# Where the context rows of the window attention are loaded, normed and transposed

## The chip, the cores and the metric

The kernel runs on one core of a Trainium2 chip. The core has five engines with instruction queues of their own: TensorE (PE in the tables; its weight loads are shown as PEld), VectorE (DVE), ScalarE (ACT), GpSimd (POOL) and SyncE (SP, which here issues loads), and 16 DMA engines that carry them. The metric is the device time of one execution in microseconds, as the median of several runs.

## The reference

The program computes two blocks of a network, one behind the other, for 256 tokens of width 1024. The first block has two layers, each a token mixing and a mixture of 16 experts. The second begins with an attention in which the 256 tokens also attend to 256 rows of a context, `ctx`. Cut to what the change touches:

```python
def rms_norm(x, g):
    y = x * rsqrt(mean(x * x, axis=-1) + EPS)
    return y * g

def grouped_moe(h, ...):                       # first block, layers 0 and 1
    for e in range(N_EXPERTS):                 # 16 experts, two per token
        he = silu(t @ w_gate[e]) * (t @ w_up[e])
        y = y + combine[:, e:e + 1] * (he @ w_down[e])

def second_block(x, c, ctx, c_ctx, ...):       # x comes from the first block
    csh1, csc1, ... = split(silu(c_ctx) @ ada_w[0] + ada_b[0], 6)
    a_lat = rms_norm(x, norm_mix[0]) * (1 + sc1) + sh1
    a_ctx = rms_norm(ctx, norm_mix[0]) * (1 + csc1) + csh1
    qc, kc, vc = qkv_heads(a_ctx, w_qkv, ...)  # keys and values of the context rows
```

`ctx` and `c_ctx` are inputs, so `a_ctx` depends on nothing that the first block computes.

## The kernel before

Activations are held with features on partitions, as `[128, 8, 256]`: eight groups of 128 features, 256 tokens. A product in full precision is made of three: `mm3` (L539 to L541) multiplies a high and a low half of weights and activations in the combinations high-high, high-low, low-high. The halves are made by a cast on ACT (`hi`, `ch`, `hh`) and a subtraction on DVE (`lo`, `cl`, `hl`).

Weights come through a rotating ring of 1 MB slots (`wtile`, `load_w`, `load_runs`); SP issues all of these loads on one queue, each in the order in which it is written, once its slot is free and the load before it on its completion lane has landed. The ring has six slots of its own and more in the mixture of experts, where `experts.ahead` lets the loads run some two experts ahead: six loads per expert, two each of `w_gate`, `w_up` and `w_down`. A scheduler sets the order on each engine from priorities and its own estimate of when data is ready; work between two branches on an expert's count of tokens (`tc.If`, one per expert) is not moved over them, so the rows between two branches hold the end of one expert and the beginning of the next.

For each expert e the loop in `moe` issues: the loads ahead; `gate_up` (32 matmuls, L1216 and L1217) on the gathered rows `xgs[g]`, which groups of four experts share; `swiglu` (`gx`); `scatter_tab` (DVE `pw`, two transposes, `PT`); and, for the expert before, `down_mm` (L1260, L1261), `weighted` (ACT writes the high half of y, DVE the low one, L1265 and L1266) and, for the one before that, `place`, a scatter into yT (L1297). Near a group's end the rows of the next group are gathered (`features`, L1199) and evicted by ACT and DVE in turns (`gained`, L1188 and L1190) into the next `xgs` tile. These tiles have two slots (tag b8). `ps_("t")` is one PSUM bank for all the small transposes, `ps_("gu")` one for gathers and gate_up.

The context rows: at the last expert `win_loads` loads them as two loads of 128 rows, with two of weights behind (L1388 to L1392). After that expert ACT squares and sums each row (L1453), two small ACT instructions give the factor, and DVE multiplies the rows by it (L1455). In `win_attention` PE transposes them in 16 pieces into four PSUM banks (L1531), ACT and DVE apply gain and shift (`cw`, L1535 and L1537), and `split_act` makes `ch` and `cl` (L451, L452), the operands of 96 context products for keys and values. The statistics of the latent's own norm stand beside them: squares of xT, products with ones (L1560) whose issue is held until the last transpose, `cosp`, `rnorm`, then `hh` and `hl` and the keys' products of the latent.

## Time and profile before

| | |
|---|---|
| median of three runs | 1836.07 us (1834.82 to 1840.8) |
| the profiled execution's own time | 1838.44 us |
| its span, first to last instruction | 1836.6 us |
| mean granted TensorE clock | 0.978 |
| PE busy | 1722.1 us, 94% of the span |
| PE weight loads | 1308.2 us, 71% |
| DVE, ACT busy | 1017.9 us (55%), 802.4 us (44%) |
| DMA | 467.33 MB, mean 254 GB/s |

Every row below is from that one profiled execution. A row of the timeline gives start, duration, engine, line and operation, what is written from what, the count of equal instructions in a row, and in square brackets how long the engine stood idle before it and who released it. Times count from the start of the span. A granted clock of 1.00 is 2.4 GHz, 0.50 is 1.2 GHz.

### The profile page before, as it was taken

The page shows a single profiled execution, that of the slowest core. Times are in us where ns is not written, and L with a number is a line of the kernel's source. Part 1 is how long each engine was busy: PE and PEld are TensorE (multiplying, and loading weights), DVE is VectorE, ACT ScalarE, POOL GpSimd, SP SyncE. Part 2 cuts the span into 40 slices and gives each one's busy share as a digit, 9 for nine tenths or more (in the row PEclk, how much of TensorE's full clock was granted, in tenths as well). Part 3 has the DMA queues.
Part 4 walks back from the last instruction along what each step waited for, and adds up shares of the span by engine and source line. Part 5 has one row for each costly group of instructions (what it writes and reads, how often), then busy time and mean ns, then how long its engine had stood idle before and what let it go on. Part 6 is the DMA issues. An engine that isn't in the chain of part 4 may idle for free. (4 is left out here: it accounts for less than half of the span.)

```text
span 1836.6 us, 30698 instructions
## 1 busy us (share of the span) xinstructions
PE 1722.1 (94%) x12565; PEld 1308.2 (71%) x12565; DVE 1017.9 (55%) x1979; ACT 802.4 (44%) x1460; POOL 6.0 (0%) x15
## 2 busy tenths in 40 slices
PE   6999998899999999999899998889999999989998
PEld 4877798444444777789444343767898998979998
DVE  4876555222222886555322222887676667667775
ACT  4544543111112654543211112777566555456663
POOL 1000000000000000000000000000000000000000
PEclk8999999999999999999899998899999999999999
DMA  9787894797799666895699996520596727585520
GB/s 325 266 275 271 294 318 154 302 414 298 297 415 360 209 223 224 293 339 198 266 413 417 414 377 209 171 94 1 206 337 239 274 92 229 184 298 185 184 92 24
DMA packets 221185, 467.33 MB, mean 254 GB/s; under 512 B 9347, under 2 KB 138353, under 8 KB 196897
## 3 DMA queue, kind: packets, MB, share of 16 engines
q1 hardware_dynamic: 219952, 462.77, 69.3%
q8 instruction: 143, 2.34, 0.5%
q10 hardware_dynamic: 656, 1.32, 0.2%
q14 instruction: 82, 0.66, 0.1%
q0 software_dynamic: 352, 0.23, 0.1%
HBM read 463.24 MB, written 1.05 MB: 253 GB/s over the span
## 5 line engine op out<-in xcount | busy, mean ns | idle before, releaser
L539 PE MATMUL mm<-hh,hi 128*128 128x256 f32 x1568 | 452.6, 289 | 10.0 <-ACT hi L520 5.1
L541 PE MATMUL mm<-hh,lo 128*128 128x256 f32 x1568 | 447.9, 286 | 1.7 <-DVE lo L521 1.6
L540 PE MATMUL mm<-hl,hi 128*128 128x256 f32 x1568 | 447.4, 285 | 1.5 <-DVE hl L463 0.7
L521 DVE TENSOR_TENSOR lo<-w,hi 128x1024 fp32r<-128x1024 f32 (+4 forms) x330 | 366.0, 1127 | 97.6 <-ACT hi L520 96.7
L520 ACT CAST hi<-w 128x1024 fp32r<-128x1024 f32 (+4 forms) x330 | 310.1, 970 | 246.9 <-PE mm L540 193.2
L539 PEld LDWEIGHTS mm<-hh,hi 128*128 128x128 f32 x1568 | 301.9, 193 | 21.9 <-ACT hi L520 7.9
L541 PEld LDWEIGHTS mm<-hh,lo 128*128 128x128 f32 x1568 | 301.7, 192 | 4.3 <-DVE lo L521 2.3
L540 PEld LDWEIGHTS mm<-hl,hi 128*128 128x128 f32 x1568 | 301.7, 192 | 4.2 <-DVE hl L463 1.6
L1216 PE MATMUL ps<-w,xg 128*64 128x512 f32 x512 | 230.8, 605 | 9.2 <-ACT xg L1188 6.9
L1217 PE MATMUL ps<-w,xg 128*64 128x512 f32 x512 | 230.9, 605 | 0.0
L1216 PEld LDWEIGHTS ps<-w,xg 128*64 128x64 f32 x512 | 69.8, 139 | 151.3 <-issue 138.7
L1234 DVE TENSOR_TENSOR gx<-gx,ps 64x512 f32<-64x512 f32 (+1 forms) x35 | 23.4, 668 | 223.6 <-ACT gx L1233 185.0
L1233 ACT ACTIVATE gx<-ps 64x512 f32<-64x512 f32 (+1 forms) x35 | 20.0, 572 | 216.0 <-PE ps L1217 213.1
L1261 PE MATMUL ps<-w,he 128*64 128x512 f32 x240 | 112.8, 610 | 0.0
L1260 PE MATMUL ps<-w,he 128*64 128x512 f32 x240 | 112.1, 609 | 0.0
L378 PE MATMUL ps<-w,crep 128*32 128x512 f32 x768 | 105.3, 604 | 2.2 <-DMA w<-in_ada_w_dram 1.4
L540 PE MATMUL yT<-zl,hi 128*128 128x256 f32 x352 | 99.3, 282 | 0.0
L541 PE MATMUL yT<-zh,lo 128*128 128x256 f32 x352 | 99.2, 282 | 0.0
L539 PE MATMUL yT<-zh,hi 128*128 128x256 f32 x352 | 99.2, 282 | 0.0
L539 PE MATMUL mm<-half,hi 128*128 128x256 f32 x320 | 93.4, 292 | 0.0
L540 PE MATMUL mm<-half,hi 128*128 128x256 f32 x320 | 91.3, 285 | 0.0
L541 PE MATMUL mm<-half,lo 128*128 128x256 f32 x320 | 90.7, 283 | 0.0
(477 smaller groups left out, 2823.6 us busy)
## 6 DMA issues: line engine op xcount, KB each, us to landing
w<-in_ada_w_dram SPq DMA_DIRECT2D x96, 1024.0 KB, 7.0
w<-in_w_gate_dram SPq DMA_DIRECT2D x64, 1024.0 KB, 11.4
w<-in_w_up_dram SPq DMA_DIRECT2D x64, 1024.0 KB, 16.2
w<-in_w_down_dram SPq DMA_DIRECT2D x60, 1024.0 KB, 10.9
w<-in_ffn_w_up_dram SPq DMA_DIRECT2D x44, 1024.0 KB, 5.2
w<-in_w_in_dram SPq DMA_DIRECT2D x36, 1024.0 KB, 8.5
w<-in_ffn_w_down_dram SPq DMA_DIRECT2D x22, 1024.0 KB, 5.6
w<-in_sc_w_in_dram SPq DMA_DIRECT2D x12, 1024.0 KB, 9.3
```

Source lines behind the costliest of these rows:

```text
L378: PE.matmul(ps[32 * g:32 * g + 32], crep[blk][:, 4 * s + g, SLOTS - 1 - i:SLOTS + 31 - i], w[i][s][:, g], start=(i + s == 0), stop=(i == n ...
L520: S.copy(hi, raw)
L521: (lo_eng or V).tensor_tensor(lo, raw, hi.bitcast(F32), OP.subtract)
L539: PE.matmul(ps, wh, ah, start=start, stop=False, skip_group_check=True)
L540: PE.matmul(ps, wh, al, start=False, stop=False, skip_group_check=True)
L541: latest[0] = PE.matmul(ps, wl, ah, start=False, stop=stop, skip_group_check=True).ins
L1216: PE.matmul(ps[0:64], xg[:, k, off:off + SL], wg[k // 4][:, k % 4], start=(k == 0), stop=(k == KD - 1), skip_group_check=True)
L1217: m = PE.matmul(ps[64:128], xg[:, k, off:off + SL], wu[k // 4][:, k % 4], start=(k == 0), stop=(k == KD - 1), skip_group_check=True)
L1233: S.activation(x_, ps[0:64], AF.Silu)
L1234: V.tensor_tensor(x_, x_, ps[64:128], OP.mult)
L1260: PE.matmul(py[0:64], he[:, j], cut(e, j, 0), start=(j == 0), stop=(j == 3), skip_group_check=True)
L1261: m = PE.matmul(py[64:128], he[:, j], cut(e, j, 1), start=(j == 0), stop=(j == 3), skip_group_check=True)
```

## The change

Four things are moved. First, the factors of the rows: `context_factors` runs in the second layer's token mixing, loads the context rows through the ring, squares and sums them on ACT, and keeps the two factors per partition in `cfac`. Second, the load of the rows themselves: at expert 12 SP loads them again into `cxt`, a tile that takes a slot of the gathered rows' tag, in two halves (rows 0 to 127, then 128 to 255), each of 512 KB in pieces of 1 KB. Third, multiplying and transposing: `context_turn(k)` for k = 0 and 1 around expert 14 and for k = 2 and 3 around expert 15 multiplies two pieces of 128x256 by the factors, transposes them in four pieces into the PSUM bank "t", and evicts them with gain and shift back into `cxt`. Fourth, `win_attention` only splits `cxt` into `ch` and `cl`; its transposes and the tie of the statistics to them are gone.

```diff
     V.memset(onec, 1.0)
 
     xT = ctile([128, KD, T], name="xT")
+    cfac = ctile([128, 2, 2], name="cfac")
+    cmod = ctile([128, KD], name="cmod")
     cols = ctile([128, ncol], name="cols")
     cact = ctile([128, 24], name="cact")
 
...
                 w = pre.pop() if pre else split_w(load_w(w_in, 0, 8, c0 + 256 * s, 256), hlp, 8)
                 return dense2(P, w, h, 8)
 
+            def context_factors():
+
+                for t in range(2):
+                    x_ = load_w(A["ctx_2"][0], 128 * t, 1, 0, D)
+                    j = H((128, 512))
+                    S.activation(j.bitcast(BF), x_[:, 0], AF.Square, accum_out=cfac[:, 0, t:t + 1])
+                rstd_of(cfac[:, 0], D, cfac[:, 1])
+
 
             R = [Obj() for _ in range(2)]
             lv = C("levels").rearrange("p (l t) -> p l t", l=7)
...
             for s in range(1, 4):
                 queries(s)
             keys_values()
+            if l:
+                context_factors()
             weave(attend(), [steps(branch_gate, n, j) for n in range(2) for j in range(2)])
             dump(f"ob{l}", ob_h[0].bitcast(F32))
 
...
             lists = {}
             placed = [None]
 
+            def context_turn(k):
+
+                for t in range(2):
+                    V.tensor_scalar(cxt[:, k, t], cxt[:, k, t], cfac[:, 1, t:t + 1], None, op0=OP.mult)
+                ps = ps_("t")
+                for i in range(2):
+                    for t in range(2):
+                        PE.transpose(ps[:, T * i + 128 * t:T * i + 128 * t + 128], cxt[:, k, t, 128 * i:128 * i + 128], ident)
+                for i in range(2):
+                    n = 2 * k + i
+                    V.tensor_scalar(cxt[:, k, i], ps[:, T * i:T * i + T], gc[:, n:n + 1], mod((1, 0), 0, n, 1), op0=OP.mult, op1=OP.add)
+                if k == 0:
+                    win_raw.append(cxt)
+
             def places(g):
 
                 lists[g] = mp.tile([128, 2, 4 * SL], F32R, name=nm("PG"), tag="PG", bufs=1)
...
                 if e == 4 and l:
                     experts.spare()
                 experts.ahead(6 * e + 14 - experts.n)
+                if l and e == NE - 4:
+
+                    cxt = mp.tile([128, 4, 2, T], F32, name="cxt", tag="b8", bufs=2)
+                    for t in range(2):
+                        nc.sync.dma_start(cxt[:, :, t], A["ctx_2"][0, 128 * t:128 * t + 128].rearrange("p (k f) -> p k f", k=4))
+                    gc = gain((1, 0), 1, "norm_mix_2", 0, None, v=1, t=cmod)
                 if l and e == NE - 1:
                     for f in win_loads:
                         rings.remove(ring)
                         rings.insert(0, ring)
                         win_raw.append(f())
                 tc.mark_branch_hint_location(f"over{l}_{e}", "LikelyTaken", [mybir.EngineType.PE])
+                if l and e >= NE - 2:
+                    context_turn(2 * (e - NE + 2))
                 w = (wts[e, 0][0::2], wts[e, 0][1::2])
                 ps = ps_("gu")
                 m = gate_up(ps, xgs[g], SL * j, w[0], w[1])
...
                     second(range(4))
                 if e:
                     weighted(py, tabs[e - 1][1], y_)
+                if l and e >= NE - 2:
+                    context_turn(2 * (e - NE + 2) + 1)
                 if g < 3 and j >= 2:
                     if j == 2:
                         places(g + 1)
...
                 mark = sp.tile([128, 1], F32, name=nm("mark"), tag="wp")
                 with tc.issue_after(S.copy(mark, he[NE - 1][:, 0, 0:1]).ins):
                     exp_ln_tables()
-
-                for t in range(2):
-                    x2 = sp.tile([128, D], BF, name=nm("x2"), tag="gxo" if t else "gx", bufs=1)
-                    rs = sp.tile([128, 2], F32, name=nm("rs"), tag="wc" if t else "po", bufs=1)
-                    S.activation(x2, win_raw[t], AF.Square, accum_out=rs[:, 0:1])
-                    rstd_of(rs[:, 0:1], D, rs[:, 1:2])
-                    V.tensor_scalar(win_raw[t], win_raw[t], rs[:, 1:2], None, op0=OP.mult)
             for h in range(2):
                 fs = slice(256 * h, 256 * h + 256)
                 py = ps_("t" if h else "y")[:, 0:256]
...
         dump(f"x_moe{l}", xT)
 
 
-    win_loads = [lambda t=t: load_w(A["ctx_2"][0], 128 * t, 1, 0, D)[:, 0] for t in range(2)]
-    win_loads += [lambda c=c: load_w(A["win_w_qkv_2"][0], 0, 8, c, 256) for c in (1024, 1280)]
+    win_loads = [lambda c=c: load_w(A["win_w_qkv_2"][0], 0, 8, c, 256) for c in (1024, 1280)]
     win_raw = []
 
     def win_attention(l, key):
...
             p0 = tc.cur_priority
             tc.cur_priority = p0 - EARLY
 
-            cx = win_raw[:2]
-            gc = gain(key, 1, "norm_mix_2", 8 * l, "gc", v=1)
-            for k in range(0, KD, 2):
-                ps = P.tile([128, 2, T], F32, name=nm("ps"), tag="ps")
-                for i in range(2):
-                    for t in range(2):
-                        turned = PE.transpose(ps[:, i, 128 * t:128 * t + 128], cx[t][:, 128 * (k + i):128 * (k + i) + 128], ident)
-                w_ = sp.tile([128, 2, T], F32, name=nm("cw"), tag="pTw", bufs=4)
-                for i in range(2):
-                    if k % 4 < CE:
-                        V.tensor_scalar(w_[:, i], ps[:, i], gc[:, k + i:k + i + 1], mod(key, 0, k + i, 1), op0=OP.mult, op1=OP.add)
-                    else:
-                        S.activation(w_[:, i], ps[:, i], AF.Identity, scale=gc[:, k + i:k + i + 1], bias=mod(key, 0, k + i, 1))
-                split_act(ch[:, k:k + 2], cl[:, k:k + 2], w_)
+            for k in range(4):
+                split_act(ch[:, 2 * k:2 * k + 2], cl[:, 2 * k:2 * k + 2], win_raw[0][:, k])
             h, hc = act(hh, hl), act(ch, cl)
             w_qkv = A["win_w_qkv_2"][0]
-            raw = win_raw[3]
-            wk = split_w(win_raw[2], hlp, 8)
+            raw = win_raw[2]
+            wk = split_w(win_raw[1], hlp, 8)
             wv = [pair(hlp, (4, 256)) for _ in range(2)]
             for i in range(2):
                 split_to(*wv[i], raw[:, 4 * i:4 * i + 4])
...
                     continue
                 if PAIR:
                     V.tensor_tensor(sq, sq, even, OP.add)
-                with tc.issue_after(turned.ins):
-                    PE.matmul(p2.rearrange("p a b -> p (a b)"), ones, sq.rearrange("p a b -> p (a b)"), start=(k == PAIR), stop=(k == KD - 1))
+                PE.matmul(p2.rearrange("p a b -> p (a b)"), ones, sq.rearrange("p a b -> p (a b)"), start=(k == PAIR), stop=(k == KD - 1))
             r1 = cosp
             rstd_of(p2[:, 0], D, r1)
             V.tensor_tensor(rnorm, r1, r1, OP.mult)
```

The scheduler spreads these steps over the rows between the branches. The first place is DVE at the start of expert 12 (between two branches; `pw` is expert 12's table, `y` expert 11's low half, `xg` the gathered rows of group 3). Before:

```order
L1242 COPY he_21706<-ps_22185 128x256
L1413 UNCONDITIONAL_BRANCH
L1208 TENSOR_SCALAR pw_22299<-PG_21636,rt 128x128 x2
L1266 SCALAR_TENSOR_TENSOR y_15505<-ps_21707,w_3363_21131,y_15504 128x512
L1190 TENSOR_SCALAR xg_21639<-ps_22201,gainp 128x256
L1190 TENSOR_SCALAR xg_21639<-ps_22212,gainp 128x256
L1234 TENSOR_TENSOR gx_22294<-gx_22294,ps_22277 64x512
L1212 TENSOR_SCALAR PT_22297<-ps_22300 128x256
```

and now, with the first multiply of `cxt`, which waits for the load of the first half:

```order
L1254 COPY he_21718<-ps_22197 128x256
L1447 UNCONDITIONAL_BRANCH
L1220 TENSOR_SCALAR pw_22315<-PG_21648,rt 128x128 x2
L1379 TENSOR_SCALAR cxt<-cxt,cfac 128x256
L1278 SCALAR_TENSOR_TENSOR y_15517<-ps_21719,w_3367_21143,y_15516 128x512
L1379 TENSOR_SCALAR cxt<-cxt,cfac 128x256 x3
L1202 TENSOR_SCALAR xg_21651<-ps_22213,gainp 128x256
L1202 TENSOR_SCALAR xg_21651<-ps_22224,gainp 128x256
L1246 TENSOR_TENSOR gx_22310<-gx_22310,ps_22293 64x512
L1224 TENSOR_SCALAR PT_22313<-ps_22316 128x256
```

The first multiply stands ahead of `y` and of both `xg`, three more stand between `y` and `xg`; the four that need the second half stand in the same way at the start of expert 13, behind its `y`.

The second place is SP at the same point, whose rows load weights of experts 13 and 14. Before:

```order
L1413 UNCONDITIONAL_BRANCH
L169 DMA w_21672<-in_w_up_dram 128x2048
L169 DMA w_22272<-in_w_gate_dram 128x2048
L169 DMA w_22264<-in_w_down_dram 128x2048
L169 DMA w_22266<-in_w_down_dram 128x2048
L169 DMA w_22268<-in_w_gate_dram 128x2048
L169 DMA w_22270<-in_w_up_dram 128x2048
```

and now:

```order
L1447 UNCONDITIONAL_BRANCH
L169 DMA w_21684<-in_w_up_dram 128x2048
L1418 DMA cxt<-in_ctx_dram 128x4x256
L169 DMA w_22284<-in_w_gate_dram 128x2048
L169 DMA w_22276<-in_w_down_dram 128x2048
L169 DMA w_22278<-in_w_down_dram 128x2048
L169 DMA w_22280<-in_w_gate_dram 128x2048
L169 DMA w_22282<-in_w_up_dram 128x2048
```

The first half of the context rows went in behind the first load, and waits for the slot of group 2's gathered rows; the second half stands behind the first load of expert 13's rows.

The third place is around expert 15. On PE, where `ps` written from `w` and `xg` is gate_up(15), now:

```order
L1447 UNCONDITIONAL_BRANCH
L1920 BRANCH_PREFETCH_HINT
L1383 MATMUL ps_23906<-cst,cxt 128x128 x4
L1228 MATMUL ps_23927<-w_22823,xg_21651 64x512
L1229 MATMUL ps_23927<-w_22825,xg_21651 64x512
L1228 MATMUL ps_23927<-w_22823,xg_21651 64x512
L1383 MATMUL ps_23920<-cst,cxt 128x128 x4
L1229 MATMUL ps_23927<-w_22825,xg_21651 64x512
```

Of before the same rows, without the two groups of four transposes:

```order
L1413 UNCONDITIONAL_BRANCH
L1905 BRANCH_PREFETCH_HINT
L1216 MATMUL ps_23888<-w_22807,xg_21639 64x512
L1217 MATMUL ps_23888<-w_22809,xg_21639 64x512
L1216 MATMUL ps_23888<-w_22807,xg_21639 64x512
```

On DVE the evictions of these groups, and the low halves `cl` made from them, stand behind expert 14's `y`, now:

```order
L1220 TENSOR_SCALAR pw_23949<-PG_21648,rt 128x128 x2
L454 TENSOR_TENSOR cl_24554<-cxt,ch_24553 128x512
L1278 SCALAR_TENSOR_TENSOR y_15517<-ps_23410,w_3634_22853,y_15516 128x512
L1386 TENSOR_SCALAR cxt<-ps_23906,cmod,mod(1, 0)_193 128x256 x2
L454 TENSOR_TENSOR cl_24554<-cxt,ch_24553 128x512
L1386 TENSOR_SCALAR cxt<-ps_23920,cmod,mod(1, 0)_193 128x256 x2
L454 TENSOR_TENSOR cl_24554<-cxt,ch_24553 128x512
L1246 TENSOR_TENSOR gx_23944<-gx_23944,ps_23927 64x512
L1224 TENSOR_SCALAR PT_23947<-ps_23950 128x256
```

The last place is PE at the start of the window attention (`mm` written from `ch`, `cl` and `hi`, `lo` are the context products, `ps` from `sq` and `ones` the statistics), now:

```order
L1498 MATMUL ps_15649<-PT_23947,y_15516 128x256 x4
L1498 MATMUL ps_15649<-PT_23947,y_15517 128x256 x4
L541 MATMUL mm_24661<-ch_24553,hi_24565 128x256
L542 MATMUL mm_24661<-cl_24554,hi_24565 128x256
L543 MATMUL mm_24661<-ch_24553,lo_24566 128x256
L1575 MATMUL ps_24581<-sq_24585,ones 128x512
L1575 MATMUL ps_24581<-sq_24593,ones 128x512
L541 MATMUL mm_24661<-ch_24553,hi_24569 128x256
L542 MATMUL mm_24661<-cl_24554,hi_24569 128x256
L543 MATMUL mm_24661<-ch_24553,lo_24570 128x256
L1575 MATMUL ps_24581<-sq_24601,ones 128x512
```

where before the 16 transposes stood between the last scatter (`ps` from `PT` and `y`) and the first product:

```order
L1469 MATMUL ps_15637<-PT_23908,y_15504 128x256 x4
L1469 MATMUL ps_15637<-PT_23908,y_15505 128x256 x4
L1531 MATMUL ps_24523<-cst,w_23879 128x128
...
L1531 MATMUL ps_24553<-cst,w_23881 128x128
L539 MATMUL mm_24659<-ch_24517,hi_24563 128x256
L539 MATMUL mm_24712<-hi_24571,ch_24517 128x256
L540 MATMUL mm_24712<-lo_24572,ch_24517 128x256
L1560 MATMUL ps_24579<-sq_24583,ones 128x512
L1560 MATMUL ps_24579<-sq_24591,ones 128x512
L540 MATMUL mm_24659<-cl_24518,hi_24563 128x256
L541 MATMUL mm_24659<-ch_24517,lo_24564 128x256
```

The transposes are gone there, and the first ones product stands behind three context products.

## Rows read from the trace of the kernel before

**Rows 1.** Window: length, busy PE, PEld, DVE, ACT, POOL; PEclk, DMA share, GB/s.

```profile
1000.00:1088.00 88.00, 82.78 (x470) 36.45 (x469) 19.96 (x43) 13.80 (x30) 0.00 (x0) 1.00 1.01 415
```

**Rows 2.** Timeline of SP's issues ahead of expert 12: start, duration of issue.

```profile
1045.96 0.43 SPq L169 DMA_DIRECT2D w<-in_w_gate_dram  x1
1046.44 0.43 SPq L169 DMA_DIRECT2D w<-in_w_up_dram  x1
1048.95 0.33 SPq L169 DMA_DIRECT2D w<-in_w_gate_dram  x1
1051.51 0.33 SPq L169 DMA_DIRECT2D w<-in_w_up_dram  x1
```

**Rows 3.** DMA issues at 1045.96, 1046.44 and 1124: KB, us to landing.

```profile
w<-in_w_gate_dram SPq DMA_DIRECT2D x1, 1024.0 KB, 17.9
...
w<-in_w_up_dram SPq DMA_DIRECT2D x1, 1024.0 KB, 20.0
...
w<-in_ctx_dram SPq DMA_DIRECT2D x2, 512.0 KB, 4.6
```

**Rows 4.** Timeline around the start of expert 12; the last row is expert 13's.

```profile
1057.46 0.59 PE L1217 MATMUL ps<-w,xg 128*64 128x512 f32 x1
...
1060.86 0.48 DVE L1208 TENSOR_SCALAR pw<-PG,rt 128x128 f32<-128x128 f32 x2
...
1064.63 0.75 DVE L1266 SCALAR_TENSOR_TENSOR y<-ps,w,y 128x512 fp32r<-128x512 f32 x1 [3.29 <-ACT y L1265]
...
1065.30 1.19 DVE L1190 TENSOR_SCALAR xg<-ps,gainp 128x256 f32<-128x256 f32 x2
1065.87 1.22 ACT L1188 ACTIVATE xg<-ps,gainp 128x256 f32<-128x256 f32 x2 [1.27 <-DVE xg L1190]
...
1066.48 0.64 PE L1216 MATMUL ps<-w,xg 128*64 128x512 f32 x1 [0.58 <-ACT xg L1188]
...
1080.60 0.75 DVE L1266 SCALAR_TENSOR_TENSOR y<-ps,w,y 128x512 fp32r<-128x512 f32 x1 [3.28 <-ACT y L1265]
```

**Rows 5.** The window attention's start: timeline, then two windows as rows 1.

```profile
1148.61 0.70 PE L1469 MATMUL ps<-PT,y 64*128 64x256 f32 x4 [0.93 <-DVE y L1464]
1153.59 3.67 PE L1531 MATMUL ps<-cst,w 128*128 128x128 f32 x16 [4.28 <-DVE xT L1472]
1157.14 0.58 PE L539 MATMUL mm<-ch,hi 128*128 128x256 f32 x1
...
1172.91 0.28 PE L541 MATMUL mm<-hi,cl 128*128 128x256 f32 x1
1173.03 0.59 PE L1595 MATMUL ps<-hs,cst 128*128 128x512 f32 x1
...
1153.50:1157.20 3.70, 3.61 (x17) 3.31 (x17) 3.47 (x8) 2.83 (x6) 0.00 (x0) 0.50 0.94 319
1157.20:1160.30 3.10, 3.10 (x9) 1.87 (x9) 2.75 (x6) 3.10 (x8) 0.00 (x0) 0.71 0.79 241
```

**Rows 6.** Timeline: transposes, gate_up(15), expert 14's y, multiply of rows, evictions.

```profile
1093.93 0.66 PE L1329 MATMUL ps<-cst,xr 128*128 128x128 f32 x4
...
1126.24 0.59 PE L1216 MATMUL ps<-w,xg 128*64 128x512 f32 x1
...
1127.23 0.75 DVE L1266 SCALAR_TENSOR_TENSOR y<-ps,w,y 128x512 fp32r<-128x512 f32 x1 [5.34 <-ACT y L1265]
...
1142.85 0.75 DVE L1455 TENSOR_SCALAR w<-w,rs 128x1024 f32<-128x1024 f32 x1 [1.79 <-DMA w<-in_win_w_qkv_dram]
...
1154.93 0.99 DVE L1535 TENSOR_SCALAR cw<-ps,gc,mod(1, 0)_191 128x256 f32<-128x256 f32 x2
```

**Rows 7.** PE's restart after expert 14's gate_up: timeline, then window.

```profile
1118.24 2.08 PE L1297 MATMUL ps<-PT,y 64*128 64x256 f32 x16 [2.14 <-issue]
...
1118.20:1124.90 6.70, 6.66 (x30) 3.60 (x32) 0.91 (x3) 0.00 (x0) 0.00 (x0) 0.50 0.16 58
```

**Rows 8.** Window in the second layer's token mixing, as rows 1.

```profile
725.00:730.00 5.00, 5.00 (x44) 4.61 (x46) 4.46 (x9) 3.40 (x6) 0.00 (x0) 1.00 0.00 0
```

## Prediction

> **What bounds the kernel now.** The page's busy shares come first: TensorE (PE) is hardly ever idle, so a change pays only where PE stands still, or costs where it makes PE stand. Then the stretches by window. Over the last experts of the second mixture, 1000 to 1088 us, PE is busy for 82.78 of 88 us and the DMA engines for all of it, 415 GB/s [rows 1]: weights stream ahead without a gap, so every load that SP issues there stands behind a queue. Next that queue: SP's issues [rows 2] beside the time from issue to landing [rows 3]. The load issued at 1045.96 lands 17.9 us later, at 1063.9; that of 1046.44 lands 20.0 later, at 1066.4: in the order of issue and 2.5 us apart, which is what 1 MB takes at 415 GB/s. Before, the context rows were loaded when the queue was empty and landed 4.6 us after issue. Last come the timelines where context work goes to and where it leaves: expert 12's start [rows 4], and the start of the window attention, where PE idles 4.28 us until DVE has written xT, runs 16 transposes in 3.67 us at half clock, and has its first context product at 1157.14 [rows 5].
>
> **Part 1, expert 12: a DVE instruction that waits for a load.** SP issues the first half of the rows (0.5 MB) right behind the w_up load of 1051.51, but must first see expert 11's gate_up end, since the tile takes the slot of group 2's gathered rows: its last matmul starts at 1057.46 and takes 0.59 [rows 2, 4]. So it is issued at about 1058.1. By the landings above, the loads of 1048.95 and 1051.51 land at 1068.9 and 1071.4; half a megabyte more takes 1.3 us: about 1072.7.
>
> In the changed order the multiply that needs it stands straight behind the two pw of expert 12. In before's time DVE is there at 1060.86 + 0.48 = 1061.34 [rows 4]. DVE's instructions start in the order in which they are written, so behind the waiting multiply stand expert 11's low half y and two evictions xg. ACT's own xg comes after DVE's first, and gate_up(12) on PE waits for ACT's; before, this chain ended at 1066.48. Now: 1072.7, one multiply 0.2 (one of 1024 columns takes 0.75 [rows 6], a quarter of that 0.19), y 0.75, three more multiplies 0.7, one xg 0.6 and ACT's xg 0.6 give 1075.6. PE loses 1075.6 - 1066.48 = **9.1 us**; the bounds are 7 (the queue 2 us shorter) and 10.5 (rows of 1 KB move at half the rate). Nothing gives it back: PE waits for no weights in this stretch, so the time only lets the loads run further ahead.
>
> After a wait PE runs at half clock. When it had stood for 2.14 us, the granted clock was 0.50 from 1118.20 to 1124.90: 6.7 us that do the work of 3.35 [rows 7]. After the 4.28 us it was 0.50 for 3.70 us and 0.71 for 3.10 us, which loses 1.85 + 0.90 = 2.75 [rows 5]. I take **+2.8** (2 to 3.4).
>
> The second half is issued once the load of 1051.51 has landed, whose successor on its completion lane it is: at 1071.4, behind the first half and six weight loads, so it lands at 1071.4 + 1.3 + 6 x 2.5 + 1.3 = 1089. Expert 13's multiplies stand behind y, which ends at 1080.60 + 0.75 = 1081.35 at before's pace [rows 4]; with the 11.9 us lost above that is 1093. No second wait: 0.
>
> **Part 2, the turns around experts 14 and 15.** Sixteen transposes in four groups; four of 128x128 take 0.66 in a busy stretch [rows 6], 0.44 of it in PE's way as they overlap their neighbours. The group ahead of gate_up(14): +0.5. Ahead of gate_up(15) one group, +0.4, then after three matmuls of gate_up(15) another, +0.4, into the same single "t" bank. That must first be evicted, and on DVE its two evictions (0.99 for two) stand behind expert 14's y, 1127.23 to 1127.98 [rows 6]. PE, whose gate_up(15) began at 1126.24, is there at about 1127.9 with the group ahead; the bank is free at 1129.0: +1.1, with the low half of the split that stands in the same row +1.5. The last group lies where PE waits for y anyway: +0.2. Together **+3.0** (1.8 to 4.3). The other evictions and multiplies lie where DVE idles ahead of a y, 5.34 us for that of expert 14: 0.
>
> **Part 3, the window attention.** Removed: 16 transposes, eight gains, and the wait of the first product for them. The first context product can start where the transposes did, at 1153.59, not at 1157.14 [rows 5]. But the half clock that then lay on the transposes now lies on products. Before, PE went from the first context product at 1157.14 to what follows the last one at 1173.03, 15.9 us [rows 5], of which the clock of 0.71 took 0.9: 15.0 at full clock for the 96 products and the ones products of the statistics among them. The half clock now takes 2.75, some 0.3 of it in waits: 1153.59 + 15.0 + 2.45 = 1171.0 in place of 1173.03: **-2.0**. The least is -1.1, since in the new order the third ones product stands behind only six products and waits for squares that ACT and DVE still make; the most, -4.5, is the full clock throughout. What is late next is the latent's own norm, whose work on ACT and DVE loses the gains and splits that stood in it, so the keys' products behind find their input.
>
> **Part 4, the last expert and the token mixing.** Squares, roots and the two multiplies leave the last expert, where they ran beside PE's last down products: 0. In the second token mixing two loads of 0.5 MB enter the ring of six slots, ahead of loads that PE needs. The DMA engines idle there from 725 to 730 us [rows 8], which would take 1 MB (2.5 us); but the loads behind move on by two slots. The ends are 0 and +3 (both loads stand in front of one that PE waits for); I take **+1**, nearer to the idle that is there.
>
> **Sum**: 9.1 + 2.8 + 3.0 - 2.0 + 1 = **+13.9**. The profiled execution took 1838.44 (its span 1836.6); with the sum 1852.3. It lies 2.37 above the median of the runs, 1836.07, so on the median's base the forecast is **1850**. The bounds: 7 + 2 + 1.8 - 4.5 + 0 = +6.3, 1842; 10.5 + 3.4 + 4.3 - 1.1 + 3 = +20.1, 1856.
>
> **Rivals.** (a) *The load lands before DVE wants it.* If the half megabyte is not held behind the queued weights, it takes its transfer of 1.3 us, or at most the 4.6 of the empty queue [rows 3], and lands between 1059.4 and 1062.7; DVE wants it at 1061.34, and the xg behind start at 1065.30 [rows 4], so nobody notices. Parts 2 to 4 remain: 3.0 - 2.0 + 1 = +2.0, **1838**. For it speaks only that half a megabyte is small; against it, that loads landed in order of issue, 2.5 us apart. The Trainium skill, page "DMA: Bandwidth & Descriptors", section "Queues, rings and completion order", says that each DMA engine takes descriptors in ring order, but that completion is not first in, first out per issuing engine; taken so far that a short late load ends ahead of long early ones, it would give this rival's time. The landings [rows 3] do not show that.
>
> (b) *Faster: the products fill PE's idle ahead of the attention.* The context products need nothing of xT. If their PSUM bank is free when the last scatter ends, at 1148.61 + 0.70 = 1149.31, they fill the 4.28 us in which the transposes waited [rows 5], the clock does not fall, and the gain is 4.3 + 2.0 = 6.3; with the load and the turns free, **1830**. It decides from the point where enough products stand ahead of the first ones product: against it, that the new order has three there, and that this ones product waits for squares of xT, which is complete only at about 1153.6. It needs (a) too.
>
> (c) *The wait moves to expert 13*: the first half in time, the second at 1089 against 1081.35; gate_up(13) hides most of it, and with some 3 us left the sum is +5, **1841**; counted with (a).
>
> **How the numbers follow.** The forecast has 0.75, (a) with (c) 0.17, (b) 0.08. A measurement of this kernel can tell about 0.3%, from 1830.6 to 1841.6 around the median: faster 0.08, same 0.17, slower 0.75. To leave out no more than 2 in 10 the range goes from the forecast's upper bound down to just below (a): 1837 to 1856.
>
> **What would show it.** Right: a DVE idle of some 11 us ahead of the first multiply of cxt, put down to the context's DMA; PE idle for about 9 us ahead of gate_up(12), against 0.58 [rows 4], and a granted clock of 0.5 behind it; the first context product about where the transposes stood after the last scatter. Wrong: a first half that lands within 5 us of its issue, no longer PE idle at expert 12, or an attention that starts its products in the idle ahead of xT.

## The result, and the profile after

The changed kernel takes **1855.03 us** (median, 1853.36 to 1856.73); the kernel before took 1838.43 (median of the three runs named at the start and one more, of 1841.12). The ratio is **1.0092, 95% interval 1.0074 to 1.0111**: slower, by 13.6 to 20.4 us. The forecast was slower, 1850 (1837 to 1856).

One table carries most of what follows. It is worked out from starts of TensorE's (PE) rows in each kernel's timeline: the first matmul of gate_up of experts 11 to 15 (e11 to e15), the last group of four scatter matmuls (S), and the first matmul behind the last context product (C; it reads `hs`). Each column is the time from one of these to the next.

```
us                 e11-e12 e12-e13 e13-e14 e14-e15  e15-S    S-C  e11-C
before               15.51   13.13   27.34   19.29  22.37  24.42 122.06
after                25.09   15.36   29.33   16.98  26.94  22.15 135.85
e4_factors           15.52   13.12   27.35   16.71  22.37  24.18 119.25
e1_late              15.52   13.13   30.52   15.86  27.06  22.13 124.22
e2_first             15.51   13.13   31.06   16.91  25.68  22.14 124.43
e6_back              15.51   13.13   33.89   14.90  25.62  22.14 125.19
e3_actq              37.48   15.41   29.27   16.89  26.99  22.13 148.17
e9_act4k             23.25   14.52   27.92   15.35  25.66  22.14 128.84
e7_fill              25.07   15.51   29.20   16.82  27.00  17.80 131.40
e5_latefill          15.52   13.12   30.17   16.66  27.02  17.79 120.28
e11_turnA            15.52   13.12   31.01   16.70  27.36  17.81 121.52
e13_turnC            15.51   13.13   31.25   16.34  29.49  18.17 123.89
e12_turnB            15.52   13.12   30.66   15.79  22.50  17.80 115.39
e14_turnB5           15.51   13.13   31.70   16.97  22.48  17.81 117.60
```

`e4_factors` has the code of before in all of this, and shows how far two executions of one code differ: not at all in e11-e13 and e15-S, 0.24 in S-C, 2.58 in e14-e15. Behind C it takes 2.4 us less.

**Expert 12.** The timeline of after (start, duration, engine, line, operation, and in brackets the idle time before it with what ended it), which answers to [rows 2] and [rows 4]:

```profile
1062.41 0.57 SPq L1418 DMA_DIRECT2D cxt<-in_ctx_dram  x1
...
1077.43 0.35 DVE L1379 TENSOR_SCALAR cxt<-cxt,cfac 128x256 f32<-128x256 f32 x1 [11.80 <-DMA cxt<-in_ctx_dram]
1077.70 0.75 DVE L1278 SCALAR_TENSOR_TENSOR y<-ps,w,y 128x512 fp32r<-128x512 f32 x1
1078.36 0.87 DVE L1379 TENSOR_SCALAR cxt<-cxt,cfac 128x256 f32<-128x256 f32 x3
1079.14 0.99 DVE L1202 TENSOR_SCALAR xg<-ps,gainp 128x256 f32<-128x256 f32 x2
...
1079.72 1.02 ACT L1200 ACTIVATE xg<-ps,gainp 128x256 f32<-128x256 f32 x2 [10.84 <-DVE xg L1202]
...
1080.34 1.11 PE L1228 MATMUL ps<-w,xg 128*64 128x512 f32 x1 [10.14 <-ACT xg L1200]
```

The whole chain can be read downward. SP issues the half megabyte at 1062.41, it lands 15.0 us later, and VectorE (DVE) stands for 11.80 us with `y` and both `xg` behind it; PE has nothing for 10.14. The windows behind it (length, busy PE, PEld, DVE, ACT, POOL; granted clock, DMA share, GB/s):

```profile
1071.00:1081.00 10.00, 0.67 (x2) 0.30 (x4) 2.70 (x7) 1.02 (x2) 0.00 (x0) 0.68 1.02 412
1081.00:1085.00 4.00, 4.00 (x12) 1.16 (x10) 0.00 (x0) 0.00 (x0) 0.00 (x0) 0.51 1.02 424
```

The DMA engines are as busy as before [rows 1]; PE restarts at half clock (0.51) for some 4 us. In the table e11-e12 grows by 9.58 and e12-e13 by 2.23.

**Experts 14 and 15.** PE's timeline around gate_up(15), against [rows 6] and [rows 7]:

```profile
1141.42 0.66 PE L1383 MATMUL ps<-cst,cxt 128*128 128x128 f32 x4
1142.01 0.64 PE L1228 MATMUL ps<-w,xg 128*64 128x512 f32 x1
1142.01 0.64 PE L1229 MATMUL ps<-w,xg 128*64 128x512 f32 x1
...
1142.92 1.02 PE L1228 MATMUL ps<-w,xg 128*64 128x512 f32 x2
1144.11 0.63 PE L1383 MATMUL ps<-cst,cxt 128*128 128x128 f32 x4 [0.18 <-DVE cxt L1386]
...
1149.87 1.02 PE L1229 MATMUL ps<-w,xg 128*64 128x512 f32 x2
1150.82 0.44 PE L1221 MATMUL ps<-cst,pw 128*128 128x128 f32 x2
1153.22 2.08 PE L1309 MATMUL ps<-PT,y 64*128 64x256 f32 x16 [1.96 <-issue]
```

Three things stand here. The second group of transposes waits only 0.18 us for the "t" bank. It also breaks up the products: L1228 and L1229 write the two halves of 64 partitions and start together (1142.01 twice); the group went in between one L1228 and its L1229, so at either end one of them runs alone, in two passes one behind the other, 1.02 in place of 0.59: 0.43 each, 0.86 together. And behind gate_up(15), at the branch on expert 15's count, PE idles for 1.96 us with nothing in the profile that it waits for ("issue"), and restarts at about half clock:

```profile
1153.20:1157.00 3.80, 3.78 (x24) 2.79 (x26) 0.42 (x1) 0.67 (x2) 0.00 (x0) 0.56 0.57 183
```

Before, such an idle stood at expert 14's branch alone [rows 7]. After has one of 2.14 there too, with less half clock behind it (0.67 over the 4.5 us from 1136.5, against 0.50 over 6.7). e15-S grows by 4.57: gate_up(15), with its two groups, is 1.85 longer, the idle adds 2.03 (before, the scatter overlapped the transposes ahead of it by 0.07), and what follows takes 0.68 more.

The other two stretches, e13-e14 with +1.99 and e14-e15 with -2.31, hold something that is not the change's. The products of expert 13's further tokens (they read `heo`) stand ahead of gate_up(14), behind the same waits of 1.06 and 0.38 us in both kernels. Before, then after:

```profile
1102.58 1.93 PE L1280 MATMUL ps<-w,heo 128*32 128x256 f32 x32 [0.38 <-DVE heo L1250]
```

```profile
1118.68 3.36 PE L1292 MATMUL ps<-w,heo 128*32 128x256 f32 x32 [0.38 <-DVE heo L1262]
```

Their clock was 1.00 before and is 0.55 now, 1.44 us more; the group of transposes ahead of gate_up(14) is the other 0.55. Before, the half clock lay on gate_up(14) instead, as this window from its start shows:

```profile
1106.95:1116.11 9.16, 9.15 (x34) 3.35 (x34) 0.75 (x1) 0.46 (x2) 0.00 (x0) 0.81 0.95 332
```

There gate_up(14) took 8.72 us, and 7.02 at full clock in after: -1.70. The half clock behind the idle is 1.20 less, and the second group adds 0.59. `e4_factors`, with before's code, has full clock on both, and so has `e9_act4k`, whose row on PE is that of after here. So 1.44, -1.70 and -1.20 are half clock that comes and goes with the execution.

**The window attention**, against [rows 5]: PE's timeline, then a window.

```profile
1168.95 0.50 PE L1498 MATMUL ps<-PT,y 64*128 64x256 f32 x4 [0.78 <-DVE y L1493]
1173.92 0.58 PE L541 MATMUL mm<-ch,hi 128*128 128x256 f32 x1 [4.47 <-DVE xT L1501]
...
1191.10 1.02 PE L1610 MATMUL ps<-hs,cst 128*128 128x512 f32 x2
```

```profile
1173.90:1177.00 3.10, 3.08 (x6) 1.88 (x7) 1.96 (x5) 2.24 (x5) 0.00 (x0) 0.50 0.88 307
```

The transposes are gone, their idle behind xT is not (4.47 against 4.28), and the half clock lies on products now. S-C falls by 2.27.

**The second token mixing.** One row at its start and gate_up(0) at its end, of before and of after:

```profile
714.45 0.39 PE L767 MATMUL lv<-half,half 128*128 128x128 f32 x2
...
889.07 0.64 PE L1216 MATMUL ps<-w,xg 128*64 128x512 f32 x1 [0.28 <-ACT xg L1188]
```

```profile
717.79 0.39 PE L777 MATMUL lv<-half,half 128*128 128x128 f32 x2
...
893.42 0.64 PE L1228 MATMUL ps<-w,xg 128*64 128x512 f32 x1 [0.28 <-ACT xg L1200]
```

3.34 late at its start, in code that the change doesn't touch, and 4.35 at its end: 1.01 lost. In the other traces of this study this start is 0.93 to 5.55 late; how much of that is drift from execution to execution is a question for `e4_factors` below. The loss in between is 0.96 to 1.15 in eleven other traces with this part of the change, `e4_factors` among them, and 3.02 in one, `e11_turnA`. In after it comes with two waits of PE:

```profile
742.85 0.65 PE L386 MATMUL ps<-cst,a 128*128 128x128 f32 x4 [0.76 <-ACT a L383]
...
744.17 0.70 PE L913 MATMUL lv<-half,half 128*128 128x256 f32 x2 [0.67 <-DVE sm L916]
```

`e4_factors` has them too, 0.76 and 0.66, and no other PE wait over the 45 us from there. Before has neither: products of a weight with the normed tokens (`mm` from `hh` and `hl`) stand ahead of and behind the same four transposes, which the scheduler has now put elsewhere. So what PE waits for here is ACT and DVE, not a load.

The account of the two profiled executions: +1.01 token mixing, +13.79 from e11 to C, -0.36 in the rest (-0.07 between, -0.29 behind C): **+14.4**, and +3.34 ahead of the token mixing's start, which gives the difference of the spans (1854.4 - 1836.6).

### The profile page after: what moved, and what is told of

It is laid out like the page before. It is cut to its first block, busy times and chain, and to the rows that moved or that the text cites. A ratio compares the mean times of both kernels' runs of the same rounds, so it can differ in the third digit from the quotient of the medians.

```text
span 1854.4 us, 30712 instructions
## 1 busy us (share of the span) xinstructions
PE 1726.9 (93%) x12565; PEld 1308.8 (71%) x12565; DVE 1021.3 (55%) x1989; ACT 801.2 (43%) x1454; POOL 6.0 (0%) x15
## 5 line engine op out<-in xcount | busy, mean ns | idle before, releaser
L1228 PE MATMUL ps<-w,xg 128*64 128x512 f32 x512 | 232.1, 607 | 17.2 <-ACT xg L1200 15.6
L1229 PE MATMUL ps<-w,xg 128*64 128x512 f32 x512 | 232.1, 607 | 0.0
L1228 PEld LDWEIGHTS ps<-w,xg 128*64 128x64 f32 x512 | 70.1, 140 | 157.0 <-issue 135.9
```

The lines of the kernel that those rows point to most:

```text
L1228: PE.matmul(ps[0:64], xg[:, k, off:off + SL], wg[k // 4][:, k % 4], start=(k == 0), stop=(k == KD - 1), skip_group_check=True)
L1229: m = PE.matmul(ps[64:128], xg[:, k, off:off + SL], wu[k // 4][:, k % 4], start=(k == 0), stop=(k == KD - 1), skip_group_check=True)
```

## Experiments

### The wait at expert 12

**e1_late** holds the multiplies of each half until the gated product of expert 12 or 13 has been taken.

```
-V.tensor_scalar(cxt[:, k, t], cxt[:, k, t], cfac[:, 1, t:t + 1], None, op0=OP.mult)
+with tc.issue_after(gx_of[NE - 4 + t]):
+    V.tensor_scalar(cxt[:, k, t], cxt[:, k, t], cfac[:, 1, t:t + 1], None, op0=OP.mult)
```

> The changed kernel, but the multiplies of the first half stand behind expert 12's gx on DVE and those of the second half behind expert 13's gx; loads, turns and the attention as changed. Theory (DVE stood behind a load in SP's queue, and y and xg stood behind DVE): the PE idle of 10.1 us ahead of gate_up(12) and the half clock after it go, 11.8 us in all; what is left is token mixing +1.0, turns +4.0, attention -2.1, so about 3 to 5 us slower than before, some 1841 where before is 1837. Rival (the extra megabyte in a saturated queue is itself the cost, wherever it is waited for): PE waits elsewhere in experts 12 to 14, for weights that land 2.5 us late, and the kernel stays over 10 us slower than before.

Measured: 1844.36, ratio 1.0026 (1.0013 to 1.0039) where after had 1.0092. Its timeline:

```profile
1069.71 0.64 PE L1228 MATMUL ps<-w,xg 128*64 128x512 f32 x1 [0.58 <-ACT xg L1200]
...
1078.65 0.35 DVE L1383 TENSOR_SCALAR cxt<-cxt,cfac 128x256 f32<-128x256 f32 x1
...
1092.22 0.35 DVE L1383 TENSOR_SCALAR cxt<-cxt,cfac 128x256 f32<-128x256 f32 x1 [0.53 <-DMA cxt<-in_ctx_dram]
...
1093.14 2.12 PE L1337 MATMUL ps<-ht,pg 128*128 128x512 f32 x8 [0.74 <-DVE pg L1331]
```

PE's idle ahead of gate_up(12) is the 0.58 of [rows 4] again, and e11-e12 and e12-e13 are those of before. The same loads, in the same place of the queue, cost nothing at expert 12 once no instruction that others need stands behind them. That settles the cause of 11.8 us of the loss. At expert 13 the same fault is left in small: the first multiply of the second half waits 0.53 us for its load with `pg` behind it, and PE waits 0.74 for `pg` (0.74 to 2.25 in the six traces with these late multiplies).

**e2_first** holds the first half alone, so that the second half's multiplies stand behind expert 13's `y`; **e6_back** issues both loads behind the six weight loads and puts all eight multiplies there.

```
-with tc.issue_after(gx_of[NE - 4 + t]):
+with nullcontext() if t else tc.issue_after(gx_of[NE - 4]):      # e2_first
```

```
+with tc.issue_after(last_load[0].ins):                           # e6_back
     nc.sync.dma_start(cxt[:, :, t], ...)
```

> The changed kernel with only the first half's multiplies held behind expert 12's gx; the second half's stay behind expert 13's y. Theory: no PE idle at expert 12; the wait moves to expert 13, as the prediction's rival (c) has it: DVE stands for some 7 us ahead of the multiplies, gx(13) comes 2 to 3 us late, and with some half clock the kernel is 3 to 5 us slower than with both held: 6 to 9 us slower than before. Rival (expert 13's gate_up hides it): as with both held, 3 to 5 us slower than before.

> The changed kernel with both loads of the context rows held behind the last of the six weight loads that are issued with them; all eight multiplies then stand behind expert 13's y. Theory (position in the queue sets the landing): both halves land at about the same point of expert 13, 18 to 23 us after their place in the queue, DVE stands 7 to 8 us ahead of the multiplies of expert 13, PE idles there for 4 us and at half clock after it: 7 to 10 us slower than before. Rival (the stall was the slot's wait, not the queue's): no wait on the load at expert 13, 3 to 5 us slower than before.

Measured: 1844.44 and 1844.5, one run each, 5.6 and 5.7 above before's 1838.83, between what theory and rival had in either. In e2_first:

```profile
1092.60 1.14 DVE L1383 TENSOR_SCALAR cxt<-cxt,cfac 128x256 f32<-128x256 f32 x4 [7.94 <-DMA cxt<-in_ctx_dram]
...
1095.61 2.14 PE L1337 MATMUL ps<-ht,pg 128*128 128x512 f32 x8 [3.13 <-DVE pg L1331]
```

A DVE wait of 7.94 becomes a PE wait of 3.13, since gate_up(13) covers the rest: the price that rival (c) gave this case. In e6_back DVE waits 6.84 and PE 3.52, near what its theory had (7 to 8, and 4). From e11 to C, however, e2_first takes 124.43 and e1_late 124.22. Of the 2.39 us that e2_first loses more at `pg` (3.13 - 0.74), 1.85 come back ahead of gate_up(14): e1_late has half clock on the products with `heo` (3.00 us, against 1.93) and on what follows. Since such half clock comes and goes in one code, one run each does not say what the place of the multiplies at expert 13 is worth at the end.

**e3_actq** issues the two loads from ACT's queue, so that they don't stand behind SP's weights.

```
-nc.sync.dma_start(cxt[:, :, t], ...)
+nc.scalar.dma_start(cxt[:, :, t], ...)
```

> The changed kernel with the two loads of the context rows issued by ACT on its own queue instead of by SP; the scheduler now puts all eight multiplies ahead of expert 12's pw. Theory (the load was late because it stood behind the weights in SP's queue): each half lands within 5 us of its issue; DVE waits for a few us, PE's idle ahead of gate_up(12) falls from 10.1 to 3 to 5 us, and the kernel is 8 to 11 us slower than before instead of 16.6. Rival (the half megabyte itself is slow while the DMA engines are saturated): 15 us to landing as on SP's queue, PE idle of 10 us or more, no gain.

Measured: 1868.28, one run. The theory was wrong, and what the rival had is nearer: the first half lands 16.6 us after its issue. The timeline, then the DMA queues from 1067 to 1073 (packets, MB, share of 16 engines; q1 is SP's, q10 ACT's):

```profile
1062.20 1.75 ACTq L1418 DMA_DIRECT2D cxt<-in_ctx_dram  x2
...
1078.76 1.14 DVE L1379 TENSOR_SCALAR cxt<-cxt,cfac 128x256 f32<-128x256 f32 x4 [13.92 <-DMA cxt<-in_ctx_dram]
...
1092.54 1.11 PE L1228 MATMUL ps<-w,xg 128*64 128x512 f32 x1 [22.54 <-ACT xg L1200]
```

```profile
q1 hardware_dynamic: 292, 2.12, 86.6%
q10 hardware_dynamic: 291, 0.30, 14.4%
```

The queues get as many packets each, 292 and 291, but SP's have 7.3 KB on average and ACT's 1 KB (2.12 MB / 292, 0.30 MB / 291). This load in a queue of its own therefore gets an eighth of the bytes, and all eight multiplies wait for it ahead of expert 12's products. The Trainium skill, page "DMA: Bandwidth & Descriptors", section "Queues, rings and completion order", says that an engine goes round the queues that have work and drains a whole packet, some 9 to 17 descriptors, from one before it goes on to the next. The equal counts agree with the taking of turns; whether what the trace counts as a packet is that page's packet no run shows.

**e9_act4k** tests that: the same, with `cxt` laid out so that a row of a load is one piece of 4 KB.

```
-cxt = mp.tile([128, 4, 2, T], F32, name="cxt", tag="b8", bufs=2)
+cxt = mp.tile([128, 2, 4, T], F32, name="cxt", tag="b8", bufs=2)
...
```

> The changed kernel with both context loads issued by ACT's queue, as in the second experiment, but into a tile laid out so that each row of a load is one piece of 4 KB where it was four of 1 KB. The eight multiplies stand ahead of expert 12's first product again, as there. Theory: two queues are served about packet by packet in turn, so the share of the context load goes by the size of its packets: 128 packets of 4 KB take as long as they and as many weight packets of 8 KB need at 415 GB/s, 1.5 MB or 3.8 us a half: issued at about 1062, landed at about 1066 and 1070, PE waits 2 to 5 us at expert 12 (22.5 with 1 KB packets), total about +8 on the kernel before, 1845 to 1849. Rival: the second queue gets a fixed small share of the bytes whatever its packets: each half takes 10 to 16 us as before, total 1862 to 1868.

Measured: 1853.0, two runs, ratio 1.0087 (1.0062 to 1.0111). Timeline, then the queues from 1069 to 1073.1, then those of the first 3.4 us behind the issue at 1064.36:

```profile
1073.06 1.14 DVE L1379 TENSOR_SCALAR cxt<-cxt,cfac 128x256 f32<-128x256 f32 x4 [6.05 <-DMA cxt<-in_ctx_dram]
1077.18 1.14 DVE L1379 TENSOR_SCALAR cxt<-cxt,cfac 128x256 f32<-128x256 f32 x4 [2.98 <-DMA cxt<-in_ctx_dram]
...
1080.47 1.12 PE L1228 MATMUL ps<-w,xg 128*64 128x512 f32 x1 [8.32 <-ACT xg L1200]
```

```profile
q1 hardware_dynamic: 156, 1.15, 68.2%
q10 hardware_dynamic: 153, 0.56, 33.8%
```

```profile
q1 hardware_dynamic: 193, 1.43, 100.3%
```

Packet for packet again (156, 153), with a third of the bytes for ACT's queue: the second half lands 4.1 us after the first, as worked out (3.8). The first takes 8.7 where I expected 4, because its queue starts late: from 1064.36 to 1067.8 it moved no packet at all beside SP's 193, and from then to 1071 it moved 116 beside 116. In e3_actq the first packet came 4.0 us after the issue; before, with the queue empty, the first packet of the context rows (issued at 1124.42) came after 1.0 us. The sharing is confirmed; that late start, which puts the time between theory and rival, I did not foresee, and no run explains it.

### The token mixing

**e4_factors** is the kernel before with `context_factors()` in the second token mixing, whose result nothing reads.

> The kernel before with one addition: the two loads, squares and roots of the context rows in the second token mixing (the changed kernel's context_factors), whose result nothing reads here. Theory: this part alone costs the +1.00 us by which every kernel with the change leaves the second token mixing later than the kernel before, and nothing else: total before + 1.0 (0.5 to 1.5, so a ratio of about 1.0005), with the whole microsecond lost between 720 and 800 us and a constant offset behind. Rival: the 2 to 3 us by which these kernels' executions are late already ahead of 700 us belong to the change too (its two small tiles and one more use of the load ring move buffers from the start on): then this kernel shows them as well, total +3 to +4.

Measured: 1836.83 against 1836.35, ratio 1.0001 (0.9988 to 1.0014): the total can't tell 1 us from 0. The trace can, with the two rows as above:

```profile
717.26 0.39 PE L777 MATMUL lv<-half,half 128*128 128x128 f32 x2
...
892.84 0.64 PE L1228 MATMUL ps<-w,xg 128*64 128x512 f32 x1 [0.28 <-ACT xg L1200]
```

2.81 late at the start, 3.77 at the end: 0.96, against 1.01 in after. The early lateness is here too, as the rival has it, but not the rival's total of +3 to +4: the interval ends at +2.6 us. So most of it is drift from execution to execution (e12_turnB and e14_turnB5, one kernel, start 2.24 and 1.51 late). That all thirteen traces with this part start later than the one trace of before leaves a smaller share of the change open.

### The window attention

**e7_fill** writes the 24 products of the context keys ahead of the latent's statistics and takes the first product's PSUM tile from a bank that the scatter does not use. The two edits were not tried apart.

```
+for tag in ('ps', 'o'):
+    P.tile([128, 2, T], F32, name=nm(tag), tag=tag)
...
+pk = dense2(P, wk, hc, 8)
...
-k1 = keys(1, hc)
+k1 = keys(1, hc, pk)
```

> The changed kernel, with two edits at the start of the window attention: the 24 products of the context keys are written ahead of the statistics of x (48 context products in a row before the first ones product), and the first product's PSUM tile lies in a bank that the tokens' scatter does not use, so it need not wait until DVE has read the last xT. Theory (the prediction's second rival as a mechanism): the 4.47 us in which PE stood behind xT fill with products, and the clock does not fall to 0.50 behind them: 4 to 5 us less than the changed kernel, about 1850.5, no PE idle over 1 us there. Rival: the latent's own chain (squares, statistics, root, normed latent, its queries) ends last in this stretch, and the products of context merely move ahead of an idle of the same size: 0 to 1 us less, with a PE idle of 3 to 5 us ahead of the products of the latent.

Measured: 1851.47, ratio 1.0083 (1.0064 to 1.0102). The medians alone do not separate it from after; the stretch does. Timeline, then a window:

```profile
1166.39 0.51 PE L1498 MATMUL ps<-PT,y 64*128 64x256 f32 x4 [0.78 <-DVE y L1493]
1166.82 0.38 PE L541 MATMUL mm<-ch,hi 128*128 128x256 f32 x1
...
1184.19 0.59 PE L1613 MATMUL ps<-hs,cst 128*128 128x512 f32 x1
```

```profile
1168.00:1171.40 3.40, 3.40 (x19) 3.40 (x18) 3.40 (x7) 2.72 (x8) 0.00 (x0) 0.50 0.81 269
```

Products follow the scatter at once and S-C is 17.80 in place of 22.15: -4.35, as the theory has it, and 17.79 to 17.81 in four of the five further traces with these edits (e13_turnC has 18.17). One point of it fell: the clock goes to 0.50 all the same, 1.2 us after the restart and for 3.4 us, while PE runs without a gap. What PE did before is two short waits, 0.56 and 0.78.

**e5_latefill** joins e1_late and e7_fill.

> The changed kernel with the late multiplies (the four multiplies of each half held behind the gated product of experts 12 and 13, as in the first experiment of this study) and with the products of the context keys ahead of the latent's statistics, from a bank of their own. Theory: both gains add: the late multiplies take 10.7 off the changed kernel (measured: 1844.4 against 1855.0) and the filled wait 4 to 5: 1839.5 to 1840.5, within 0.1% of the kernel before. Rival: what the late multiplies leave, a latent chain that bounds the attention, takes the fill's gain: 1843.5 to 1844.5.

Measured: 1840.79, ratio 1.0015 (1.0001 to 1.0028). From e11 to C it takes 120.28, 4 less than e1_late: both gains stand. What is left against before stands in e15-S, 27.02 against 22.37, and in e13-e14, 30.17 against 27.34.

### The turns and the idle at the branch

Three kernels place the four groups of transposes of e5_latefill otherwise: ahead of gate_up(14), ahead of gate_up(15), and in the last expert's part.

```
-if l and e >= NE - 2:
-    context_turn(2 * (e - NE + 2))
+if l and e == NE - 2:              # all three; in e13_turnC only context_turn(0)
+    for k in (0, 1):
+        context_turn(k)
+if l and e == NE - 1:              # e12_turnB alone
+    context_turn(2)
...
-if l and e >= NE - 2:
-    context_turn(2 * (e - NE + 2) + 1)
+if l and e == NE - 1:              # (3,) in e12_turnB, (1, 2, 3) in e13_turnC
+    for k in (2, 3):
+        context_turn(k)
```

> The kernel with late multiplies and filled wait (1840.8), with the four turns placed otherwise: the first two groups ahead of gate_up(14), none around gate_up(15), two behind expert 14's y in the last expert's part. Theory: the groups around gate_up(15) cost 2.1 us of transposes in the row of products and, by making PE's sequencer late at the branch behind it, the idle of 1.98 us that the profile calls issue and the half clock behind that, together 4.2 us at expert 15. Without them gate_up(15) takes 7.0 us as before, the idle is gone there, and the moved groups cost 0.5 each: 3 us less, 1837.5 to 1838.5. Rival: the idle at that branch comes from elsewhere and stays, or goes to the branch of expert 14: then 0.5 to 1 us less, 1840 to 1841.

> As the previous one, but two groups ahead of gate_up(14), one ahead of gate_up(15) and one in the last expert's part. Theory (the groups ahead of a branch make the sequencer late): a single group may leave some of the idle, between 0 and 1.98 us, at expert 15. Rival (it doesn't hang on the groups): the idle of about 2 us is there with one group as with two or none.

> As the previous two, but one group ahead of gate_up(14), none around gate_up(15), three in the last expert's part. Theory: as with none around gate_up(15) in the first of these three, no idle at expert 15; the third group in the last part stands behind the scatter, where PE waits for y and xT anyway, but its eviction and split stand late, so the filled wait reopens by up to 1 us: 1836.5 to 1838.5. Rival: the groups in the last part delay the last scatter by 0.5 each, and the context products wait for the last chunk: 1840 or more.

Measured: e11_turnA (2, 0, 2) 1839.82, ratio 1.0014 (1.0001 to 1.0028); e12_turnB (2, 1, 1) 1832.5, one run; e13_turnC (1, 0, 3) 1843.28, ratio 1.0026 (1.0015 to 1.0038). My theory fell: e11_turnA has no group around gate_up(15) and an idle of 2.18 there, as its rival has it, and e12_turnB has one and 0.39. e13_turnC, too, comes out where its rival has it. In e13_turnC, three groups in the last part, PE waits 4.34 us for the last `y`, ahead of which DVE now has 4.62 us of weight splits (e15-S 29.49).

**e14_turnB5** is e12_turnB again, the kernel that its expectation calls that of the twelfth experiment, to see what one program does from execution to execution.

> The kernel of the twelfth experiment once more, unchanged (late multiplies, filled wait, turns placed 2, 1 and 1), with many executions, since it had one (1832.5) and that one showed no idle over 0.4 us at the branches of experts 14 and 15. Theory 1: the 2 us idles are fixed by the program (where its instructions stand), so this program has none: the second profile shows 0.1 to 0.5 us at both branches again, median 1831.5 to 1834, about 0.9975 of the kernel before. Theory 2: they come and go between executions of one program, as its executions' times fall into groups some microseconds apart: the profile shows about 2 us at one of the branches, or not, and the median is 1835 to 1838, 0.9985 to 1.0005 of the kernel before.

Measured: 1835.89 against 1839.0, ratio 0.9988 (0.9974 to 1.0002), 12 runs: the median that theory 2 gave. The trace shows reads of 0.02 MB by queues that it calls instruction queues. At the branch of expert 15, first e11_turnA with its timeline and the queues of 0.2 us from 1139.1, then e14_turnB5, where such a read begins at 1136.00:

```profile
1139.26 0.44 PE L1221 MATMUL ps<-cst,pw 128*128 128x128 f32 x2
1141.88 0.39 PE L1311 MATMUL ps<-PT,y 64*128 64x256 f32 x2 [2.18 <-issue]
```

```profile
q8 instruction: 1, 0.02, 36.1%
```

```profile
1137.78 0.44 PE L1221 MATMUL ps<-cst,pw 128*128 128x128 f32 x2
1138.70 1.21 PE L1311 MATMUL ps<-PT,y 64*128 64x256 f32 x16 [0.49 <-ACT gx L1247]
```

The same for both branches, with the kernels' first names (how long before the end of the matmuls ahead of the branch a read began, by the start of its packet in the trace; time from that start to PE's restart; idle):

```
expert 14:  before 0.42, 2.56, 2.14   after 0.49, 2.63, 2.14   e13 0.47, 2.58, 2.12
            e4 -0.01, 2.60, 2.60      e5 0.82, 2.59, 1.77      e12 2.43, 2.59, 0.16
            e14 4.33, -, none         e1 3.78, -, none
expert 15:  after 0.76, 2.72, 1.96    e5 0.74, 2.72, 1.98      e1 0.76, 2.72, 1.96
            e11 0.53, 2.71, 2.18      e12 2.32, 2.70, 0.39     e14 2.22, 2.70, 0.49
```

Where PE idles, it restarts 2.56 to 2.63 us (expert 14) or 2.70 to 2.72 (expert 15) after such a read began, and the idle is what is left of that behind the branch. (The profile puts some of these idles down to the end of an ACT instruction, as in the last row above, but the scatter reads nothing of `gx`.) Before at expert 15, e11 at 14 and e13 at 15 have a read 0.1 to 0.4 ahead and no idle; the trace does not say for which engine a read is, so the link is supported and not shown. The Trainium skill, page "Runtime: NRT & Kernel Launch", section "Instruction fetch mechanics", says that instructions come in blocks of 16 KiB and that a taken branch out of the blocks at hand waits for a read; the rows fit that. Theory 1 holds at expert 15 (0.39 and 0.49 in two executions of one program; 1.95 to 1.98 in the kernels with two groups there). At expert 14 it does not: e12 and e14 are one program, with 0.16 and none, and e1 and e5 have the same instructions up to there, with none and 1.77. The median, too, speaks against it (1831.5 to 1834 by theory 1). Why a read starts when it does stays open.

From e11 to C this kernel takes 115.39 and 117.60, before's code 122.06 and 119.25: 4.2 less on average, 3 with the token mixing's microsecond off, which is within the interval. Against the kernel before it is the same or up to 0.26% faster; no gain can be claimed.

## Why the prediction was right

- **Part 1, the wait at expert 12** (9.1 + 2.8 = 11.9): 9.58 + 2.23 = 11.81. Issue forecast at 1058.1 on before's clock, found at 1062.41 - 4.28 (the lateness of gate_up(11)) = 1058.13; landing forecast at 1072.7, found at 1073.15; the second half, forecast at 1089, lands at 1092.22 in e1_late, whose lateness is 3.2: 1089.0. In after its multiplies wait for nothing: no second wait, as forecast. e1_late shows that the wait is the cause.
- **Part 2, the turns** (+3.0, 1.8 to 4.3): 1.99 - 2.31 + 4.57 = +4.25, in the bounds and by other terms than given. The first three groups cost 0.55 + 0.59 + 1.85 = 2.99, where the sum had 0.5 + 0.4 + 1.9. But the step on the "t" bank failed: PE waits 0.18 for it in place of 1.5, since its three products ahead take 1.93 us (1142.01 to 1143.94), where the forecast has PE there some 1.2 after their start. Of the 1.85, 0.86 are the broken pairs, which are not in the sum. Nor are the idle at expert 15's branch (2.03) and the 0.68 behind it; half clock that comes and goes takes 1.46 off again (1.44 - 1.70 - 1.20). That the whole came out near the forecast is in part luck.
- **Part 3, the attention** (-2.0): -2.27. Transposes out, half clock on the products, the idle behind xT left: all as forecast.
- **Part 4** (+1): 1.01, and 0.96 with that part alone: the size is right, and by luck. The forecast priced two loads in front of one that PE waits for; the traces show no wait for a load there, but waits of 0.76 for ACT and 0.67 for DVE, where the scheduler had moved the products that stood between. The last expert's part, forecast at 0, can't be read apart from part 2.
- **The sum** (+13.9): +14.4 in the traces, 13.6 to 20.4 by the ratio's interval. The median lies 5 above the forecast of 1850; of that 2.4 is the base (before's median is 1838.43 with the fourth run, and was 1836.07 with three).
- **The rivals.** (a) fell: the half lands 15.0 us after its issue, in its turn; a queue of its own made it worse. (c)'s price was right at expert 13 in e2_first (3.13); what of it reaches the end one run can't tell. (b)'s mechanism is real and was not in this change: with e7_fill's order and bank it gives 4.35, where (b) had 4.3 for the filled idle; (b)'s clock that does not fall was wrong, it fell to 0.50 there too.

## What to carry to other kernels

An instruction that waits for a DMA is priced by what stands behind it on its engine: follow that row to PE before placing it, and hold it behind the instructions that PE's next products need; here this took 11.6 us off the stretch from e11 to C, and where one multiply still stood ahead of such an instruction, at expert 13, PE lost 0.74 us and more. A load moved to another queue under full load took its share by packets here, so its pieces have to be about as long as those it competes with, and its first packet came 3.5 us and more after the issue. A term of a sum that comes out right is checked by the wait that makes it up: the microsecond of the token mixing was forecast from loads and was made of waits for ACT and DVE. Transposes put between products should not stand inside a pair that runs side by side.

## What the runs showed of the hardware that I had not expected

- Two queues under load were served packet for packet (292 and 291; 156 and 153), so the bytes went by packet size; the second queue moved its first packet only 3.5 and 4.0 us after the issue, against 1.0 in an empty queue.
- Two matmuls that write different halves of 64 partitions start together (0.59 us for both); apart, two of a kind take 1.02.
- PE's granted clock fell to 0.50 for 3.4 us although PE had been running without a gap for 1.2 us, behind waits of 0.56 and 0.78.
- Half clock behind the same row of short waits (1.06, 0.38, 0.66, 0.77) fell on one group of products, on the next or on none, in executions of the same code: 1.1 to 1.7 us each time.
- A branch can cost PE 2 us with no wait in the profile, and a read of 0.02 MB of instructions had begun 2.56 to 2.72 us before each such restart.
